# Sum of reciprocals: five of the first ten loads move from SyncE's queue to ScalarE's

## The chip, the cores and the metric

The kernel runs on one core of a Trainium2 chip. Its time is the device time of one execution in microseconds, taken as the median of several runs. Engines are named as in the profile: PE is TensorE, DVE is VectorE, ACT is ScalarE, POOL is GpSimd, SP is SyncE. SP computes nothing here; it issues DMA transfers.

## The reference

```python
def setup_inputs():
    batch, seq, dim = 32, 512, 1024
    return {"x": np.abs(np.random.randn(batch, seq, dim)).astype(np.float32) + 1e-6}

def reference(x):
    return np.sum(1.0 / x, axis=-1).astype(np.float32)
```

The input has 16384 rows of 1024 float32 numbers (67.1 MB). The output is one float32 number for each row, the sum of the reciprocals of its elements.

## The kernel before

The 16384 rows are laid out as 128 partitions with 128 rows each, so "row c" below means one row in each partition, a tile of 128x1024. All data goes through `ring`, a buffer in SBUF of R = 40 such rows. `LOADS` (line 42) lists the 26 transfers that fill it: ten loads of 8 rows (4 MB each, numbered 0 to 9 here), eight loads of 4 rows (2 MB) and eight of 2 rows (1 MB). The ring therefore holds five of the big loads: load 5 goes to the place of load 0, load 7 to that of load 2, load 9 to that of load 4. A load may be issued only when all readers of the rows that stood in its place are done.

Each load is cut into chunks of two rows. The kernel uses 1/a + 1/b = (a + b) / (a b): of a row it multiplies the left half by the right half (512 products), takes the reciprocals of the products as Exp(-Ln(product)) on ACT, and multiplies them by the sums of the two halves. The products are made by POOL (line 141), mostly two rows at a time; in a chunk of kind C one of the two rows is done by PE and DVE instead (lines 129 and 130). ACT then runs one Ln (line 152) and one Exp (line 156 or 162) for each chunk. For chunks of kind A, DVE multiplies the whole row by the reciprocals, repeated for both halves, and adds up (line 92). For kinds B and C, PE first adds the two halves into PSUM (line 148, `add`, line 82), and DVE multiplies that by the reciprocals and adds up (line 92). An even big load is A, B, A, B; an odd one is A, B, A, C. So POOL has four operations on two rows in an even load, and three and a half in an odd one.

DVE's sums of a chunk are issued one chunk late: `waiting` holds them until the next chunk's products have been issued (line 150), and the last sums of a load come with the first chunk of the next load.

`keep` pins the order in which instructions were written on their engine. In the version before, every load is issued by SP at the top of its turn of the loop (line 122), in the order of use. SP runs far ahead: loads 0 to 4 need no free place and are issued at once; later ones wait for their place. The output (64 KB) is written by one transfer at the end (line 169).

Of the kernel before, what the change touches and what calls it, by code (L numbers as in the profile page):

```python
# [1 line left out]

# [6 lines left out]


@with_exitstack
def kernel(
    ctx: ExitStack,
    tc: tile.TileContext,
    x: bass.AP,
    out: bass.AP,
):

    nc = tc.nc
    f32 = mybir.dt.float32
    P = 128  # L30
    D = 1024
    H = D // 2
    F = 128

    R = 40

    S = float(2**17)

    A, B, C = (2, 0, 0), (2, 2, 0), (2, 2, 1)
    LOADS = [[A, B, A, B], [A, B, A, C]] * 5 + [[A, B], [A, C]] * 4 + [[A], [B], [A], [C]] * 2

    Ln = mybir.ActivationFunctionType.Ln
    Exp = mybir.ActivationFunctionType.Exp
    mult = mybir.AluOpType.mult
    plus = mybir.AluOpType.add

    x_v = x.flatten_outer_dims().rearrange("(p f) d -> p f d", p=P)
    out_v = out.flatten().rearrange("(p f) -> p f", p=P)  # L50

    act_sets = list(get_activation_tables(nc.m.arch).keys())
    nc.scalar.add_instruction(  # L53
        mybir.InstLoadActFuncSet(
            name=nc.get_next_instruction_name(),
            act_func_set_id=act_sets.index("natural_log_exp_and_others"),
            ins=[],
            outs=[],
        )
    )  # L60

    ppool = ctx.enter_context(tc.tile_pool(name="ppool", bufs=4))
    opool = ctx.enter_context(tc.tile_pool(name="opool", bufs=1))
    spool = ctx.enter_context(
        tc.tile_pool(name="spool", bufs=3, space=bass.MemoryType.PSUM)
    )
    bpool = ctx.enter_context(
        tc.tile_pool(name="bpool", bufs=1, space=bass.MemoryType.PSUM)
    )
    rpool = ctx.enter_context(  # L70
        tc.tile_pool(name="rpool", bufs=2, space=bass.MemoryType.PSUM)
    )

    ring = opool.tile([P, R, D], f32)
    sums = opool.tile([P, F], f32)
    ident = opool.tile([P, P], f32)
    make_identity(nc, ident)
    keep = tc.keep_in_program_order

    def add(bank, *halves):  # L80
        for k, half in enumerate(halves):
            i = nc.tensor.matmul(  # L82
                bank,
                lhsT=ident,
                rhs=half,
                start=k == 0,
                stop=k == len(halves) - 1,
            )
            keep(i)

    def sum_row(c, row, fac, out=None):
        i = nc.vector.tensor_tensor_reduce(  # L92
            out=row if out is None else out,
            in0=row,
            in1=fac,
            scale=S,
            scalar=0.0,
            op0=mult,
            op1=plus,
            accum_out=sums[:, c : c + 1],  # L100
        )
        keep(i)

    def sum_rows(c, xc, pr, sm, rc):
        m, e = xc.shape[1], len(sm)
        for j in range(e, m):
            row = xc[:, j, :].rearrange("p (h e) -> p h e", h=2)
            sum_row(
                c + j,
                row,  # L110
                rc[:, j - e, :].unsqueeze(1).to_broadcast([P, 2, H]),
                pr[:, e : e + 2, :] if j == e and m - e > 1 else None,
            )
        for j in reversed(range(e)):
            sum_row(c + j, pr[:, j, :], sm[j])

    waiting = None
    c0 = 0
    for chunks in LOADS:
        n = sum(m for m, _, _ in chunks)  # L120
        xt = ring[:, c0 % R : c0 % R + n, :]
        keep(nc.sync.dma_start(out=xt, in_=x_v[:, c0 : c0 + n, :]))  # L122

        made, q = [], 0
        for m, e, v in chunks:
            pr = ppool.tile([P, m, H], f32, tag="ps" if e else "pr")
            for j in range(v):
                b = bpool.tile([P, H], f32, tag="b")
                add(b, xt[:, q + j, H:])
                i = nc.vector.tensor_tensor(  # L130
                    out=pr[:, j, :], in0=xt[:, q + j, :H], in1=b, op=mult
                )
                keep(i)
            made.append(pr)
            q += m

        q = 0
        for (m, e, v), pr in zip(chunks, made):
            xc = xt[:, q : q + m, :]
            if v < m:  # L140
                i = nc.gpsimd.tensor_tensor(  # L141
                    out=pr[:, v:, :], in0=xc[:, v:, :H], in1=xc[:, v:, H:], op=mult
                )
                keep(i)
            sm = []
            for j in range(e):
                s = spool.tile([P, H], f32, tag="s")
                add(s, xc[:, j, :H], xc[:, j, H:])
                sm.append(s)
            if waiting:  # L150
                sum_rows(*waiting)
            keep(nc.scalar.activation(out=pr, in_=pr, func=Ln, scale=S))  # L152
            rc = None
            if e < m:
                rc = rpool.tile([P, m - e, H], f32, tag="rc")
                i = nc.scalar.activation(  # L156
                    out=rc, in_=pr[:, e:, :], func=Exp, scale=-1.0
                )
                keep(i)
            if e:  # L160
                r = pr[:, :e, :]
                keep(nc.scalar.activation(out=r, in_=r, func=Exp, scale=-1.0))  # L162
            waiting = c0 + q, xc, pr, sm, rc
            q += m
        c0 += n
    assert c0 == F, c0
    sum_rows(*waiting)

    nc.sync.dma_start(out=out_v, in_=sums)


# [1 line left out]
_INS = ['x']  # L173
_OUTS = [((32, 512), 'float32')]


# [23 lines left out]
```

## Time and profile before

| what | value |
|---|---|
| median of 3 runs | 171.74 us (171.68 to 172.3) |
| the profiled execution | 171.68 us |
| its span, first to last instruction | 169.9 us |
| mean granted TensorE clock | 0.998 |
| moved by DMA | 67.24 MB, 396 GB/s over the span |
| a load of 4 MB, from issue to landing | 37.8 us (median of ten) |

The page gives busy times of the engines, then the span in 40 slices (each digit the busy share in tenths), the DMA queues, and the chain of work that ended last, followed back from the end. A line of a timeline gives start, duration, engine, source line, the operation with its output and inputs, how many were merged, and in square brackets the idle time before it with what ended it. A line of an answer by windows gives the window, its length, then for PE, its weight loads, DVE, ACT and POOL the busy time and number of instructions, the granted clock, the busy share of the DMA engines, and GB/s. Times are microseconds from the start of the span.

### The profile page before, as it was taken

Reading aid. Unit: us, or ns where it says so; the run is one execution under the profiler, and the core shown is the slowest. Engines: PE = TensorE matmul, PEld = TensorE weight load, DVE = VectorE, ACT = ScalarE, POOL = GpSimd, SP = SyncE. Lnnn points to the kernel's source line nnn. Section 1 sums busy time; section 2 is a strip of 40 time slices with the busy share of each in tenths; the row PEclk is TensorE's granted clock in tenths of the full one; section 3 lists DMA queues with packets and bytes.
Section 4 is the critical chain, followed back from the end, with each engine's and each line's share of the span. In section 5 each row is a group of like instructions: output and inputs, shape, how many; then the busy total and the mean of one; then the engine's idle time right before and its main releaser. Section 6 shows DMA issues by size and latency. Waiting matters only on the chain.

```text
span 169.9 us, 1267 instructions
## 1 busy us (share of the span) xinstructions
PE 131.7 (77%) x278; PEld 50.5 (30%) x278; DVE 122.3 (72%) x267; ACT 133.9 (79%) x129; POOL 138.3 (81%) x70
## 2 busy tenths in 40 slices
PE   0008999786988789784997869789999999888790
PEld 0003433331332233231432323224334342333230
DVE  0000777767987577767777679778989898889883
ACT  3002989978887987958889787999999988999890
POOL 1008999699996999689996998999999889998920
PEclk9999999999999999999999999999999999999999
DMA  6999999999999999999999999999999999999400
GB/s 208 409 455 409 463 409 455 409 463 401 463 411 447 424 440 420 432 434 424 440 424 440 424 397 434 424 428 426 432 428 432 424 413 417 422 420 424 187 0 15
DMA packets 3894, 67.24 MB, mean 396 GB/s; under 512 B 432, under 2 KB 560, under 8 KB 560
## 3 DMA queue, kind: packets, MB, share of 16 engines
q1 hardware_dynamic: 3888, 67.18, 92.9%
q8 instruction: 2, 0.03, 0.1%
q14 instruction: 4, 0.03, 0.0%
HBM read 67.11 MB, written 0.07 MB: 395 GB/s over the span
## 4 chain that ended last, share of the span: by engine, by line
DMA 78%; POOL 11%; DVE 3%; ACT 2%; issue 2%; SPq 1%; POOLq 0%; DVEq 0%
DMA ring<-in_x_dram 78%; POOL pr L141 11%; DVE pr L92 2%; DVE ring L92 1%; ACT pr L152 1%; ACT rc L156 1%; SPq L122 1%; POOLq L141 0%; DVE sums L92 0%; DVEq L92 0%; DVEq L195 0%
## 5 line engine op out<-in xcount | busy, mean ns | idle before, releaser
L141 POOL TENSOR_TENSOR pr<-ring 128x1024 f32<-128x1024 f32 x64 | 137.6, 2189 | 23.6 <-DMA ring<-in_x_dram 23.3
L82 PE MATMUL s<-ring,ident 128*128 128x512 f32 x256 | 122.4, 616 | 32.5 <-DVE sums L92 16.6
L152 ACT ACTIVATE pr<-pr 128x1024 f32<-128x1024 f32 x64 | 67.4, 1053 | 28.7 <-POOL pr L141 28.5
L82 PEld LDWEIGHTS s<-ring,ident 128*128 128x128 f32 x256 | 47.0, 194 | 105.3 <-issue 63.1
L92 DVE CUSTOM_DVE_ANT_1 pr<-ring,rc 128x1024 f32<-128x1024 f32 x32 | 39.1, 1221 | 44.6 <-ACT rc L156 44.6
L92 DVE CUSTOM_DVE_ANT_0 pr<-pr,s 128x512 f32<-128x512 f32 x64 | 41.3, 683 | 0.2
L92 DVE CUSTOM_DVE_ANT_1 ring<-ring,rc 128x1024 f32<-128x1024 f32 x32 | 38.9, 1216 | 0.0
L162 ACT ACTIVATE pr<-pr 128x1024 f32<-128x1024 f32 x32 | 33.8, 1058 | 1.0
L156 ACT ACTIVATE rc<-pr 128x1024 f32<-128x1024 f32 x32 | 32.9, 1028 | 1.0
L82 PE MATMUL b<-ring,ident 128*128 128x512 f32 x22 | 12.0, 626 | 1.4 <-DMA ring<-in_x_dram 1.4
L92 DVE DVE_READ_ACCUMULATOR2_ANT sums<- 128x1 f32 x128 | 10.6, 83 | 0.0
L130 DVE TENSOR_TENSOR pr<-ring,b 128x512 f32<-128x512 f32 x11 | 7.5, 683 | 0.1
L82 PEld LDWEIGHTS b<-ring,ident 128*128 128x128 f32 x22 | 3.5, 188 | 9.0 <-DMA ring<-in_x_dram 7.6
L53 ACT ACT_TABLE_LOAD x1 | 1.3, 1283 | 0.7 <-PEq L184 0.7
masks.py:197 POOL MEMSET ident<- 128x128 f32 x1 | 0.2, 204 | 0.3 <-POOLq L184 0.3
masks.py:199 POOL TENSOR_SCALAR_AFFINE_SELECT ident<-ident 128x128 f32<-128x128 f32 x1 | 0.3, 292 | 0.1
L184 POOL MEMSET const-float32-0.0<- 128x1 f32 x1 | 0.1, 98 | 0.2 <-issue 0.2
L184 POOL MEMSET const-uint8-127<- 128x1 uint8 x1 | 0.1, 103 | 0.0
L184 POOL MEMSET const-bfloat16-1.0<- 128x1 bf16 x1 | 0.1, 101 | 0.0
L184 POOL MEMSET const-float32-1.0<- 128x1 f32 x1 | 0.1, 98 | 0.0
## 6 DMA issues: line engine op xcount, KB each, us to landing
ring<-in_x_dram SPq DMA_DIRECT2D x10, 4096.0 KB, 37.8
ring<-in_x_dram SPq DMA_DIRECT2D x8, 2048.0 KB, 37.0
ring<-in_x_dram SPq DMA_DIRECT2D x8, 1024.0 KB, 28.3
out_dram<-sums SPq DMA_DIRECT2D x1, 64.0 KB, 1.5
```

The lines of the kernel that those rows point to most:

```text
L53: nc.scalar.add_instruction(mybir.InstLoadActFuncSet(name=nc.get_next_instruction_name(), act_func_set_id=act_sets.index("natural_log_exp_ ...
L82: i = nc.tensor.matmul(bank, lhsT=ident, rhs=half, start=k == 0, stop=k == len(halves) - 1,)
L92: i = nc.vector.tensor_tensor_reduce(out=row if out is None else out, in0=row, in1=fac, scale=S, scalar=0.0, op0=mult, op1=plus, accum_out ...
L122: keep(nc.sync.dma_start(out=xt, in_=x_v[:, c0 : c0 + n, :]))
L130: i = nc.vector.tensor_tensor(out=pr[:, j, :], in0=xt[:, q + j, :H], in1=b, op=mult)
L141: i = nc.gpsimd.tensor_tensor(out=pr[:, v:, :], in0=xc[:, v:, :H], in1=xc[:, v:, H:], op=mult)
L152: keep(nc.scalar.activation(out=pr, in_=pr, func=Ln, scale=S))
L156: i = nc.scalar.activation(out=rc, in_=pr[:, e:, :], func=Exp, scale=-1.0)
L162: keep(nc.scalar.activation(out=r, in_=r, func=Exp, scale=-1.0))
L184: nc = _bacc.Bacc("TRN2", target_bir_lowering=False, num_devices=1)
```

## The change

Of the first `OTHER` = 10 loads, the odd ones are issued by ACT (`nc.scalar`) instead of SP. They are issued `AHEAD` = 3 turns of the loop before their use: loads 1 and 3 at the top of turn 0, load 5 at the top of turn 2, load 7 at turn 4, load 9 at turn 6. The even ones and all loads from number 10 on stay on SP, each at the top of its own turn as before. What is loaded, and where to, is the same. The sums on DVE are not touched by the diff.

```diff
+    AHEAD, OTHER = 3, 10
...
+    first = [0]
+    for chunks in LOADS:
+        first.append(first[-1] + sum(m for m, _, _ in chunks))
+
+    def load(eng, a):
+        r0, n = first[a], first[a + 1] - first[a]
+        i = eng.dma_start(
+            out=ring[:, r0 % R : r0 % R + n, :], in_=x_v[:, r0 : r0 + n, :]
+        )
+        keep(i)
+
     waiting = None
     c0 = 0
-    for chunks in LOADS:
+    for k, chunks in enumerate(LOADS):
         n = sum(m for m, _, _ in chunks)
         xt = ring[:, c0 % R : c0 % R + n, :]
-        keep(nc.sync.dma_start(out=xt, in_=x_v[:, c0 : c0 + n, :]))
+
+        ahead = range(k, k + AHEAD + 1) if k == 0 else (k + AHEAD,)
+        for a in ahead:
+            if a < OTHER and a % 2:
+                load(nc.scalar, a)
+        if k >= OTHER or k % 2 == 0:
+            load(nc.sync, k)
```

## The prediction

> **What bounds the kernel now.** I read the page first: busy shares, the slices, the queues and the chain that ended last.
>
> ```profile
> span 169.9 us, 1267 instructions
> PE 131.7 (77%) x278; PEld 50.5 (30%) x278; DVE 122.3 (72%) x267; ACT 133.9 (79%) x129; POOL 138.3 (81%) x70
> ...
> POOL 1008999699996999689996998999999889998920
> ...
> DMA  6999999999999999999999999999999999999400
> ...
> q1 hardware_dynamic: 3888, 67.18, 92.9%
> ...
> DMA 78%; POOL 11%; DVE 3%; ACT 2%; issue 2%; SPq 1%; POOLq 0%; DVEq 0%
> ```
>
> All input goes through one queue, q1. It keeps the 16 DMA engines busy from the first slice to the 37th. The chain is DMA for 78% and ends in POOL, then the short ACT and DVE tail. POOL (line 141) is the busiest engine at 81%, so I next read the timeline of POOL, in three windows, which shows what each load gives it (start, us, then what ended the idle time before):
>
> ```profile
> 13.45 9.31 POOL L141 TENSOR_TENSOR pr<-ring 128x1024 f32<-128x1024 f32 x4 [12.15 <-DMA ring<-in_x_dram]
> 23.14 8.27 POOL L141 TENSOR_TENSOR pr<-ring 128x1024 f32<-128x1024 f32 x4 [0.38 <-DMA ring<-in_x_dram]
> 32.92 9.34 POOL L141 TENSOR_TENSOR pr<-ring 128x1024 f32<-128x1024 f32 x4 [1.52 <-DMA ring<-in_x_dram]
> ...
> 52.66 9.32 POOL L141 TENSOR_TENSOR pr<-ring 128x1024 f32<-128x1024 f32 x4 [1.76 <-DMA ring<-in_x_dram]
> ```
> ```profile
> 73.05 9.33 POOL L141 TENSOR_TENSOR pr<-ring 128x1024 f32<-128x1024 f32 x4 [2.42 <-DMA ring<-in_x_dram]
> 82.77 8.28 POOL L141 TENSOR_TENSOR pr<-ring 128x1024 f32<-128x1024 f32 x4 [0.39 <-DMA ring<-in_x_dram]
> 92.48 9.34 POOL L141 TENSOR_TENSOR pr<-ring 128x1024 f32<-128x1024 f32 x4 [1.43 <-DMA ring<-in_x_dram]
> ```
> ```profile
> 102.54 32.97 POOL L141 TENSOR_TENSOR pr<-ring 128x1024 f32<-128x1024 f32 x16 [0.72 <-DMA ring<-in_x_dram]
> ```
>
> Each of the first ten loads (numbered 0 to 9, 4 MB each) starts a row here. They come about 9.71 us apart (13.45, 23.14, 32.92). POOL needs 9.32 us for an even load (four operations, 2.33 each) and 8.27 for an odd one (three, and one of 1.25). So POOL is 0.4 to 2.4 us early for each next load: the stage is bound by DMA, and POOL needs 4% less time than DMA for an even load and 15% less for an odd one. From 102.54 on sixteen operations run without a wait, 12 x 2.33 + 4 x 1.25 = 32.96 us: there POOL's own pace shows. ACT in that stretch also runs without gaps, at 2.06 us for each chunk, or 8.25 us for four; POOL needs 8.24. Both keep that pace, and nothing else is slower.
>
> The last POOL operation ends at 162.50 and the span at 169.94; the 7.4 us between are tail and output. The profiled execution took 171.68 us, 1.74 more than its span, and the median of the runs is 171.74, so 171.68 is the base of my sum.
>
> **How a second queue would be served.** No row of this trace has two queues full at once, but one has a foreign packet among q1's. This is the DMA view of 62 to 74 us, while load 6 comes in:
>
> ```profile
> q1 hardware_dynamic: 171, 5.08, 98.5%
> q8 instruction: 1, 0.02, 0.6%
> ```
>
> By the packet records, q1 moves each load as eight pieces of 32768 bytes on each engine, 1.213 us a piece (8 x 1.213 = 9.70, the spacing above). The q8 packet starts at 66.05 us, some 3.7 us into load 6, and the next q1 piece on that engine starts at 67.09. So an engine leaves a load after three of its eight pieces and serves the other queue. I therefore take it that two full queues alternate piece by piece. That q1 piece then took 1.72 us instead of 1.21.
>
> The Trainium skill, page "DMA: Bandwidth & Descriptors", section "Queues, rings and completion order", says that an engine goes round its queues and switches only at packet boundaries, a packet being typically 9 to 17 descriptors. A load has eight pieces and one completion record on each engine, so by that figure whole loads might alternate and the time would stay at 171.7. The row inside load 6 speaks for the finer turn, and by it the sum is the one below.
>
> **The change, part by part.**
>
> Issues on ACT. Five loads leave SP for ACT. SP's issues last 0.327 to 0.919 us each, so ACT gains 1.6 to 4.6 us in all. Loads 1 and 3 go out before any data is there, when ACT has only its table load (0.73 to 2.01). Loads 5, 7 and 9 stand ahead of loads 2, 4 and 6's first Ln, where ACT will be waiting for data; I cost them at nothing. Without that cover it would be at most 0.9 us each. Their waits for a free slot are also free: in the trace SP sends load 5 at 25.14, 2.4 us after POOL's last operation on load 0, whereas ACT reaches its issue a whole load later. Behind it on ACT stand only the Lns of the next load, and VectorE behind them. On SP, loads 2 and 4 no longer stand behind 1 and 3; load 6 still waits for load 1's slot. Nothing else on SP, PE, POOL or DVE moves.
>
> Landing times. SP starts load 0 at 0.74 and its first piece runs at 1.75. ACT issues load 1 at about 2.0, and its pieces start about 1 us later. From there the pieces of loads 0 and 1 take turns. Load 0 needs its own eight pieces and waits for 6 or 7 of load 1's, so it lands 6.5 x 1.213 = 7.9 us later than now: at 21.3 instead of 13.45. Load 1 lands one piece later than now, about 24.3. The same holds for each pair (2,3) to (8,9), since the engines move the same bytes at the same rate: even loads land 7.9 us late, odd loads 1.2.
>
> POOL with these landings (start is the later of landing and the end before):
> - load 0: 21.3 to 30.7; load 1: to 38.9
> - load 2: 32.92 + 7.9 = 40.8 to 50.1; load 3: to 58.4
> - load 4: 60.6 to 69.9; load 5: to 78.2
> - load 6: 81.0 to 90.3; load 7: to 98.6
> - load 8: 92.48 + 7.9 = 100.4 to 109.7; load 9: to 118.0
>
> ACT finishes a load about 2.3 us after POOL, so it issues load 5 at about 41.2, load 7 at 60.7, load 9 at 80.5, each 2.5 us or more before the load ahead on its queue ends (43.9, 63.6, 84.0). Both queues stay fed, and the pairing goes on to load 9.
>
> The rest. After load 9 there are 24 POOL operations: 18 x 2.33 + 6 x 1.25 = 49.4 us, ending at 167.4. The data for them is there: the last load lands at 161.1 now and keeps its place, and POOL would want it at 166. Slots come free in time too, as SP's next loads need those of loads 5 to 8. So POOL ends 167.4 - 162.5 = 4.9 us later. Of the 7.9 us, 3.0 come back: 0.7 us is POOL's wait before load 9 that vanishes (with the rounding of the rows), and 2.3 us are its waits in the small loads at the end (162.5 less 102.54 + 8.26 + 49.4 = 160.2). The tail is unchanged. **171.68 + 4.9 = 176.6 us.**
>
> Two unknowns: the turn (6 or 7 pieces, 0.6 us each way), and a loss at a switch of queues. Its ends: zero, since a switch between two full queues may overlap; or the 0.51 us by which the piece after q8's was long. I take near zero, since that piece followed a lone packet; 2% loss would put load 8 at 102.3 and the time at 178.5.
>
> **Rivals.**
> 1. Whole loads alternate, or the engines take loads in order of need: then load 0 lands at 13.4 as now and everything stays. 171.7 us. Against it is the q8 packet inside load 6.
> 2. Engines empty SP's queue first. Loads 0, 2, 4 land at 13.4, 23.1, 32.9; load 1 at 42.6, load 3 at 52.5. POOL starts load 1 at 42.6, then runs 1 to 9 without a wait (5 x 8.27 + 4 x 9.32 = 78.6) to 121.3, then 49.4 to 170.7: 8.2 us more, 180 us.
> 3. The switch costs its full 0.5 us at every piece: 1.72 us a piece, load 8 at about 3.7 + 78.5 x 1.72 = 139, then 67 us of POOL: over 210 us. Half a loss is enough to leave my range. Nothing but two lone packets speaks for it.
> 4. Faster: 9.71 us a load is the limit of one queue, and two draw more. It decides from about 5% more rate, where load 8 lands at 95.5 and POOL ends at 162.5; at 10% POOL alone binds (about 20 + 137.2), and the time is 167. Against it is this answer on the first stretch, with DMA share 1.00 and 432 GB/s in its last columns:
>
> ```profile
> 13.40:23.10 9.70, 9.59 (x16) 4.02 (x16) 4.12 (x9) 6.60 (x7) 9.31 (x4) 1.00 1.00 432
> ```
> The engines have no idle time that a second queue could fill.
>
> **How the numbers follow.** Alternation by pieces 0.76 (176.6; its own range 174.8 to 179.5), whole loads 0.08, SP first 0.06, a large loss at switches 0.06, more rate 0.04. A measurement of this kernel tells about 0.5% (0.9 us) from no change. Faster 0.04, same 0.08, slower 0.88. The range takes in the bounds of the alternation and the SP-first case and leaves out the ends: 174.8 to 181.
>
> **What would show it.** A second dynamic queue with five of the loads; POOL's first operation at about 21 us instead of 13.45; POOL's rows of loads 0 and 1, 2 and 3 joined, with waits of 1.8 to 2.5 us before each even load only; no wait on DMA after about 100 us; q1 and the new queue together still near 430 GB/s until 160 us. It is wrong if load 0 still lands near 13.4, if POOL waits for an odd load, if the DMA rate in the first 100 us is off 430 by more than 2%, or if another engine stops POOL after 118 us.

## The result, and the profile after

The changed kernel takes 173.76 us (median; 173.53 to 173.88), the kernel before 171.98 us in the same comparison. The ratio is 1.0102, with a 95% interval of 1.0076 to 1.0127: slower by 1%, in the direction that was forecast, but by 1.8 us where 4.9 were forecast, and below the stated range. The profiled execution took 173.79 us with a span of 172.1, which is 2.1 us more than the profiled execution before on both counts.

The page of the changed kernel, its lines that answer to those of before:

```profile
span 172.1 us, 1264 instructions
...
POOL 1000069995999999999999699999999999999920
...
DMA  6999999999999999999999999999999999999000
...
q1 hardware_dynamic: 3168, 46.20, 63.5%
q10 hardware_dynamic: 720, 20.97, 28.3%
...
DMA 44%; ACT 25%; POOL 13%; issue 9%; DVE 7%; SPq 0%; POOLq 0%; DVEq 0%; ACTq 0%
```

A second dynamic queue, q10, carries five loads (20.97 MB). The DMA engines are as full as before and done at the same time (the last load lands at 161.07 us, before at 161.06), though the span is longer. What changed is the end of the chain: DMA carries 44% of it instead of 78%, and ACT, POOL and DVE have taken over, since at the end the data is there before the engines want it. POOL's digits show two more empty slices at the start. Its timeline shows the rest (start, us, and in brackets the wait before):

```profile
23.14 17.53 POOL L159 TENSOR_TENSOR pr<-ring 128x1024 f32<-128x1024 f32 x8 [21.83 <-DMA ring<-in_x_dram]
42.63 35.10 POOL L159 TENSOR_TENSOR pr<-ring 128x1024 f32<-128x1024 f32 x16 [1.97 <-DMA ring<-in_x_dram]
78.14 9.35 POOL L159 TENSOR_TENSOR pr<-ring 128x1024 f32<-128x1024 f32 x4 [0.41 <-DMA ring<-in_x_dram]
87.66 8.29 POOL L159 TENSOR_TENSOR pr<-ring 128x1024 f32<-128x1024 f32 x4 [0.18 <-DMA ring<-in_x_dram]
97.42 66.99 POOL L159 TENSOR_TENSOR pr<-ring 128x1024 f32<-128x1024 f32 x32 [1.47 <-DMA ring<-in_x_dram]
```

The rows start with loads 0, 2, 6, 7 and 8. Load 0 is late by 9.7 us (23.14 instead of 13.45) and load 8 by 4.9 us (97.42 instead of 92.48). After load 8 POOL works for 67 us without a wait and ends at 164.40, 1.9 us later than before (162.50). The rest of the 2.1 us is the tail.

That load 4 has no row of its own is what the prediction did not have: it landed while POOL was still busy. The reason stands in three views. First, ACT's first two issues, in its timeline of the first 5 us:

```profile
0.73 1.28 ACT L54 ACT_TABLE_LOAD   x1 [0.73 <-PEq L202]
0.76 0.87 ACTq L124 DMA_DIRECT2D ring<-in_x_dram  x2
```

ACT issued loads 1 and 3 from 0.76 on, beside its table load and not after it. By the packet records load 1's first pieces ran at 3.6 to 4.5, directly behind the first pieces of load 0, and from there the two loads took turns. Both landed together, at 23.06 and 23.24. With POOL 1.8 us later than predicted, ACT came later to the issue of load 5:

```profile
42.59 1.06 ACT L180 ACTIVATE pr<-pr 128x1024 f32<-128x1024 f32 x1
42.65 0.34 ACTq L124 DMA_DIRECT2D ring<-in_x_dram  x1
```

By then its queue was empty: load 3's completion records (packets of 4 bytes, one behind the eight pieces on each engine) had run at 41.1 to 42.1. Here is the DMA view of 30 to 40 us, and after it that of 42.7 to 46 us:

```profile
q10 hardware_dynamic: 67, 2.20, 50.8%
q1 hardware_dynamic: 64, 2.10, 48.5%
```
```profile
q1 hardware_dynamic: 43, 1.41, 98.9%
```

At 30 to 40 us the two queues share evenly. From 42.7 to 46 us SP's queue has the engines to itself. The packet records put the first piece of load 5 at 46.1 us on the first engine and at 48.0 on the last, 3.5 to 5.3 us after its issue. In this gap load 4, on SP's queue, got ahead: it landed at 58.3 instead of beside load 5 (67.1).

### The profile page after: what moved, and what is told of

It reads as the page before. It is cut to its first block, busy times and chain, and to the rows that moved or that the text cites. A ratio compares the mean times of both kernels' runs of the same rounds, so it can differ in the third digit from the quotient of the medians.

```text
span 172.1 us, 1264 instructions
## 1 busy us (share of the span) xinstructions
PE 129.5 (75%) x278; PEld 51.0 (30%) x278; DVE 121.9 (71%) x267; ACT 133.3 (77%) x129; POOL 138.0 (80%) x70
## 3 DMA queue, kind: packets, MB, share of 16 engines
q10 hardware_dynamic: 720, 20.97, 28.3%
## 4 chain that ended last, share of the span: by engine, by line
DMA 44%; ACT 25%; POOL 13%; issue 9%; DVE 7%; SPq 0%; POOLq 0%; DVEq 0%; ACTq 0%
DMA ring<-in_x_dram 44%; ACT pr L170 15%; POOL pr L159 13%; ACT pr L180 6%; ACT rc L174 4%; DVE pr L93 3%; DVE ring L93 3%; DVE pr L148 1%; DVE sums L93 0%; SPq L124 0%; POOLq L159 0%; DVEq L93 0%; ACTq L170 0%; DVEq L213 0%
## 5 line engine op out<-in xcount | busy, mean ns | idle before, releaser
L83 PE MATMUL b<-ring,ident 128*128 128x512 f32 x22 | 11.3, 595 | 0.0
L83 PEld LDWEIGHTS b<-ring,ident 128*128 128x128 f32 x22 | 4.1, 190 | 5.4 <-issue 4.8
```

What stands on the lines that cost most here:

```text
L83: i = nc.tensor.matmul(bank, lhsT=ident, rhs=half, start=k == 0, stop=k == len(halves) - 1,)
```

## The experiments

The ratios are to the kernel before in the same series (171.78 us for the first four experiments, 171.89 us for the last three). The theory after the result, "sharing": two full queues take turns piece by piece, so that of two loads that share the engines, the one needed first lands late. What this costs is set by the last late landing alone: its time plus the POOL work that is then left. The rivals: "start", the late first load costs, and is won back at some rate; and "issue", the five issues hold up ACT.

**One turn earlier.** Load 5 goes out at the top of turn 1, 7 at turn 3, 9 at turn 5, so that ACT's queue does not run dry.

```diff
-    AHEAD, OTHER = 3, 10
+    AHEAD, OTHER = 4, 10
```

> ScalarE issues its loads one turn earlier (load 5 at the top of turn 1), so its queue should not run dry. Theory 'sharing' (two full queues take turns piece by piece; what counts is how late load 8 lands, then 67 us of POOL): loads 4, 6 and 8 land with their partners, load 8 at 101 to 102 us instead of 97.3, time 177 to 178.4 us, slower than the changed kernel. Rival 'start' (the first load's 10 us delay is what costs, and is won back at a fixed rate): start unchanged, 173.8. Rival 'issue' (the issues hold up ACT): 173.8 or less, as they go out earlier.

Measured 178.45 us, ratio 1.0388 (1.0373 to 1.0403). POOL's timeline:

```profile
23.18 17.53 POOL L159 TENSOR_TENSOR pr<-ring 128x1024 f32<-128x1024 f32 x8 [21.88 <-DMA ring<-in_x_dram]
42.67 17.57 POOL L159 TENSOR_TENSOR pr<-ring 128x1024 f32<-128x1024 f32 x8 [1.96 <-DMA ring<-in_x_dram]
62.32 17.58 POOL L159 TENSOR_TENSOR pr<-ring 128x1024 f32<-128x1024 f32 x8 [2.09 <-DMA ring<-in_x_dram]
82.69 17.56 POOL L159 TENSOR_TENSOR pr<-ring 128x1024 f32<-128x1024 f32 x8 [2.79 <-DMA ring<-in_x_dram]
102.12 66.94 POOL L159 TENSOR_TENSOR pr<-ring 128x1024 f32<-128x1024 f32 x32 [1.87 <-DMA ring<-in_x_dram]
```

This is the pattern that the prediction drew for the changed kernel: a pair every 19.4 to 20.4 us, 17.6 us of POOL for each, a wait before every even load. The start is the same as in the changed kernel, 23.18 us, and the time is 4.7 us longer, as load 8 comes at 102.12 instead of 97.42. ACT's queue did not run dry here: load 5 was issued at 34.79, and its first pieces ran at 42.3 to 43.3, at the next turn behind load 3. Both rivals expected 173.8 or less.

**Load 1 alone through ACT, and all but load 9.**

```diff
-    AHEAD, OTHER = 3, 10
+    AHEAD, OTHER = 3, 2      # only load 1
```
```diff
-    AHEAD, OTHER = 3, 10
+    AHEAD, OTHER = 3, 8      # loads 1, 3, 5, 7
```

> Only load 1 goes through ScalarE; all others stay on SyncE. Theory 'sharing': loads 0 and 1 both land near 23.1 us, POOL then works without a wait on what is already there (23.1 + 137.2 = 160.3 is below the old end of 162.5), and the end is again set by the last landing: 171.7 to 172.2, no loss, though POOL starts 10 us late. Rival 'start': the whole loss, 173.5 to 174. Rival 'issue': a fifth of it, 172.1.

> Loads 1, 3, 5, 7 go through ScalarE, load 9 stays on SyncE, so that load 8 is not shared. Theory 'sharing': the last late even load is load 6, at about 78 us; 78.1 + 84.4 us of POOL left = 162.5, the old end: 171.8 to 172.4. Rival 'start': 173.8 as for the full change. Rival 'issue': four fifths of the loss, 173.4.

Measured 171.67 us, ratio 0.9995 (0.9986 to 1.0004), for load 1 alone, and 172.23 us, ratio 1.0033 (1.0019 to 1.0046), for all but load 9. POOL's timeline with load 1 alone:

```profile
23.23 112.36 POOL L159 TENSOR_TENSOR pr<-ring 128x1024 f32<-128x1024 f32 x52 [21.93 <-DMA ring<-in_x_dram]
136.57 4.69 POOL L159 TENSOR_TENSOR pr<-ring 128x1024 f32<-128x1024 f32 x2 [0.98 <-DVE sums L93]
```

POOL starts 9.8 us late and the kernel loses nothing: 52 operations then run in one go, with none of the waits of before, and by 136.57 POOL is where it was before (136.45). The view puts that last wait down to DVE, but the load that this row reads landed at 136.44, the last thing to come. Without load 9 on ACT, the last late landing is load 6, and the row after it runs to the end:

```profile
78.34 84.49 POOL L159 TENSOR_TENSOR pr<-ring 128x1024 f32<-128x1024 f32 x40 [0.37 <-DMA ring<-in_x_dram]
```

78.34 + 84.49 = 162.83, 0.3 us after the old end. "Start" expected the full loss in both and falls. So moves 1 to 4 cost 0.5 us of the 1.8, and the fifth costs the rest.

**Load 9 alone through ACT.**

```diff
-            if a < OTHER and a % 2:
+            if a == 9:
                 load(nc.scalar, a)
-        if k >= OTHER or k % 2 == 0:
+        if k != 9:
             load(nc.sync, k)
```

> Only load 9 goes through ScalarE, at the top of turn 6; the start is untouched. Theory 'sharing': load 9 takes every other piece from loads 7 and 8; load 7 lands near 88 us instead of 82.6 and load 8 near 101 instead of 92.4; POOL ends near 168.5: 177 to 178.5, worse than the full change with one fifth of its moves. Rival 'start': 171.7. Rival 'issue': 172.1.

Measured 178.50 us, ratio 1.0396 (1.0382 to 1.0409). One move of the five costs 6.7 us, nearly four times as much as all five together. The rows of loads 7 and 8 in POOL's timeline:

```profile
86.32 8.23 POOL L159 TENSOR_TENSOR pr<-ring 128x1024 f32<-128x1024 f32 x4 [4.03 <-DMA ring<-in_x_dram]
102.10 66.92 POOL L159 TENSOR_TENSOR pr<-ring 128x1024 f32<-128x1024 f32 x32 [7.55 <-DMA ring<-in_x_dram]
```

Load 9 landed at 99.5, ahead of load 8 (102.0), which is needed before it. Its first piece ran at 78.9 us. In the changed kernel it ran at 85.0, since load 9 stood behind load 7 on ACT's queue, and SP's queue had its head start from the gap at 42 us; so load 8 came at 97.42 there. Load 9's issue on ACT took 3.15 us in this run:

```profile
72.72 3.15 ACTq L124 DMA_DIRECT2D ring<-in_x_dram  x1
```

"Issue", which expected a fifth of the loss, falls here all the same: POOL's waits before loads 7 and 8 are for data, and 102.10 + 66.92 = 169.02, the last late landing plus the POOL work left, is 6.5 us past the old end.

**Smaller pieces on ACT's queue.**

```diff
-        i = eng.dma_start(
-            out=ring[:, r0 % R : r0 % R + n, :], in_=x_v[:, r0 : r0 + n, :]
-        )
-        keep(i)
+        step = 4 if eng is nc.scalar else n
+        for q in range(r0, r0 + n, step):
+            i = eng.dma_start(
+                out=ring[:, q % R : q % R + step, :], in_=x_v[:, q : q + step, :]
+            )
+            keep(i)
```

> As the changed kernel, but ScalarE's loads go out as two transfers of 4 rows (pieces of 16384 bytes, 0.614 us, instead of 32768, 1.213 us). Theory 'turns by piece': load 0 needs 8 x (1.213 + 0.614) us and lands near 18.3 us instead of 23.1, and load 1, with a third of the bytes, near 33 instead of 23.2. Load 3, which then needs 16 turns beside loads 4 and 6, lands near 60, POOL waits for odd loads, and the time is 176 to 183. Rival 'turns by bytes' (both queues get half the rate): load 0 at 23.1, load 1 at 23.2, time near 173.8.

Measured 177.05 us, ratio 1.0308 (1.0291 to 1.0325). Load 0 landed at 18.10 us, the second half of load 1 at 32.87 and that of load 3 at 61.93. POOL's timeline:

```profile
18.18 13.94 POOL L161 TENSOR_TENSOR pr<-ring 128x1024 f32<-128x1024 f32 x6 [16.87 <-DMA ring<-in_x_dram]
32.94 12.91 POOL L161 TENSOR_TENSOR pr<-ring 128x1024 f32<-128x1024 f32 x6 [0.82 <-DMA ring<-in_x_dram]
47.63 4.67 POOL L161 TENSOR_TENSOR pr<-ring 128x1024 f32<-128x1024 f32 x2 [1.78 <-DMA ring<-in_x_dram]
62.00 105.61 POOL L161 TENSOR_TENSOR pr<-ring 128x1024 f32<-128x1024 f32 x50 [9.70 <-DMA ring<-in_x_dram]
```

The turn is by piece and not by bytes. With pieces half as long, ACT's queue gets a third of the rate; load 0 is 5 us less late, and load 3 becomes the late one (62.00, a wait of 9.70). 62.00 + 105.61 = 167.61 is again the last late landing plus the POOL work left.

**Small loads in place of the five.** All loads as before on SP; the issues on ACT are there, but move 32 KB each.

```diff
+    tiny = opool.tile([P, 5, 64], f32)
...
+    TINY = {0: (0, 1), 2: (2,), 4: (3,), 6: (4,)}
+    for k, chunks in enumerate(LOADS):
...
+        for a in TINY.get(k, ()):
+            keep(nc.scalar.dma_start(out=tiny[:, a, :], in_=x_v[:, 0, a * 64 : a * 64 + 64]))
```

> The kernel before, with all loads on SyncE, and five small loads (256 bytes in each partition, to a place that nobody reads) issued by ScalarE at the places where the changed kernel issues its five. Theory 'sharing': the issues themselves cost nothing: 171.7 to 172.1. Rival 'issue': the loss of the changed kernel, 173.5. Beside the time it shows how long a second queue waits for its turn while the first is full: about 3.5 to 8 us from issue to the first piece, if it is as for loads 5 and 9 of the earlier runs, or under 1.3 us, one piece of load, if the wait there had another reason.

Measured 172.48 us, ratio 1.0034 (1.0022 to 1.0047): a little above "sharing", far below "issue". The 0.6 us are on the DMA side: load 9 landed at 102.9 us instead of 102.05, so 40 small pieces on each engine cost it about 0.9 us, 0.02 each. POOL waited 24.2 us for loads, against 23.3 before, which is the same 0.9 us. The view puts 23.2 of them down to DMA, and one wait to DVE:

```profile
137.35 4.70 POOL L145 TENSOR_TENSOR pr<-ring 128x1024 f32<-128x1024 f32 x2 [1.04 <-DVE sums L93]
```

But the load that this row reads landed at 137.22, and before the same wait (0.94) stood under DMA. The DMA issues show what a second queue goes through:

```profile
tiny<-in_x_dram ACTq DMA_DIRECT2D x5, 32.0 KB, 14.0
```

A load of 32 KB took 14.0 us from issue to landing (median of five). The one issued at 33.64 has its first piece at 37.13, then its eight pieces on each engine go out one for each of SP's packets, until 44.5 to 46.0, and its completion records at 45.8 to 47.2. A packet of SP's is a piece, 1.2 us, or the completion record of load 3: at about 42 us, on each engine, one small piece runs just before that record and one just after it. So a record takes a turn of its own.

**One turn later.**

```diff
-    AHEAD, OTHER = 3, 10
+    AHEAD, OTHER = 2, 10
```

> ScalarE issues its loads one turn later than in the changed kernel (load 3 at the top of turn 1, load 5 at turn 3, load 7 at 5, load 9 at 7). Theory 'sharing': the even loads now get ahead, but the odd ones come late: load 3 is issued near 35 us, gets its first piece near 39 and lands near 57, while POOL is done with load 2 at 50; a wait of 5 us or more before each odd load, and the time is over 178. Rival 'earlier is worse, later is better' (a straight line through the two leads tried, 178.4 at four turns and 173.8 at three): about 171.7 or less.

Measured 180.57 us, ratio 1.0503 (1.0474 to 1.0532). Load 3 landed at 56.75 and load 7 at 95.72:

```profile
56.89 35.10 POOL L159 TENSOR_TENSOR pr<-ring 128x1024 f32<-128x1024 f32 x16 [7.02 <-DMA ring<-in_x_dram]
95.85 75.14 POOL L159 TENSOR_TENSOR pr<-ring 128x1024 f32<-128x1024 f32 x36 [3.87 <-DMA ring<-in_x_dram]
```

Here odd loads are late, 3 and 7. The expectation of 5 us or more before each odd load held for load 3 alone: load 7 cost a wait of 3.87, loads 5 and 9 none. The sum holds again: 95.85 + 75.14 = 170.99 at the end of POOL. Of the three leads tried (178.45, 173.76 and 180.57 us for four, three and two turns) the middle one is best: with the longer one the even loads are late, with the shorter one the odd ones. No version with a second queue was faster than the kernel before.

## Why the prediction was right and wrong

**The turn by pieces was right.** The queues alternate by pieces of 32768 bytes, as read from the lone q8 packet (evenly at 30 to 40 us, and one for one in the run with small pieces). An estimate from the typical figure of the Trainium skill, page "DMA: Bandwidth & Descriptors", section "Queues, rings and completion order", would have given whole loads in turn. The runs show single pieces in turn, and the measurement decides. There is no loss at a switch between full queues worth the name: in the run one turn earlier load 9 lands at 102.2, before at 102.05, though all ten loads were interleaved. The issues on ACT cost nothing that a run shows. The sum after load 8 was exact: predicted 67.0 us of POOL, measured 66.99, 66.94 and 66.92 in three kernels, and the tail unchanged within 0.2 us.

**The landing of load 8 was wrong**, 100.4 predicted, 97.42 measured. The error of the time, 176.6 less 173.79 in the profiled execution, is these 3.0 us less the 0.2 of the tail. It comes from two terms of the step on landing times:

- The turn was mis-sized. Load 0 was to be 6.5 x 1.213 = 7.9 us late; it was 9.7 us late, eight pieces, and POOL started 1.8 us later than predicted. I counted the 6 or 7 pieces of load 1 that run ahead of load 0's last piece. It was 7, and the completion record of load 0 waits a turn as well: on all 16 engines load 1's eighth piece ran between the two (on the first engine load 0's last piece started at 19.34, load 1's at 20.55, the record at 21.76), and load 0 landed only after the last of these records. I also had ACT's issue late, at about 2.0 instead of 0.76; what this was worth by itself, no run shows. The run one turn earlier has load 8 at 102.12, 1.7 us above my 100.4.
- "Both queues stay fed" was false. I counted 1 us from ACT's issue to the first piece, taken from SP's first load, which met idle engines. Behind a full queue it was 3.4 us or more. I put the issue of load 5 at 41.2, 2.5 us or more before load 3's end. It came at 42.65, because POOL ran 1.8 us later; and with 3.5 to 5.3 us more to its first piece it would have missed even from 41.2. ACT's queue stood empty for about four pieces, SP's queue took them all, and the even loads kept that lead: load 8 came 4.7 us sooner than in the run whose queue stayed fed.

1.7 - 4.7 = -3.0 us, the difference between 97.42 and 100.4. The two errors partly cancel, which is luck. The first alone would have left the time in my range, as the run one turn earlier shows (178.45). The step that failed is "Both queues stay fed, and the pairing goes on to load 9": my range had taken in a turn 0.6 us off and a loss of rate, both with a pairing that holds. It had no term for a queue that runs dry, and that made it too high.

The signs that the prediction named held in part: the first operation came at 23.1 instead of 21, loads 0 and 1 and loads 2 and 3 were joined, and there was no wait for DMA after about 100 us; but load 4 had no wait, and the odd load 7 had one of 0.18 us.

## What to carry to other kernels

Here one queue already kept the DMA engines full, and a second added no rate (432 GB/s from 60 to 97 us, 429 before). It changed the order in which data landed: a load needed later took turns with the one needed now. Price such a change by the last late landing plus the work of the slowest engine that is left after it, not by the sum of the waits: a start 10 us later cost nothing here, and one load near the end cost 6.7 us. Before counting on two queues in step, look at when each next issue is reached, and add the time that a new load waits while the other queue is full.

## What the runs showed of the hardware

- A load on an empty queue, issued while the other queue was full, had its first piece on the earliest engine 3.4 to 3.6 us after the start of its issue in seven cases (load 5 in the changed kernel and in the run without load 9 on ACT, the three later small loads, and loads 3 and 7 in the run one turn later), and 6.2 us after it in one (load 9 alone). On idle engines it was 1.0 us. What the engines do in that time, no run here shows. In the eighth case the issue itself was long, 3.15 us, where the seven others took 0.33 to 0.34; from the end of the issue it is 3.0 to 3.3 us in all eight. Why this one issue was long is open.
- A load's completion record takes a turn of its own between two full queues (the records of load 0 at 21.8 to 22.7 us in the changed kernel, each behind the other load's last piece).
- In the run with load 9 alone, the late queue then caught up: from 79.4 to 84.3 us it started 42 pieces to the other's 23, before the two went evenly. Why is open.
- ACT issued DMAs while its table load ran (0.76 to 1.63 within 0.73 to 2.01).
